# Closing products of the SSD head pairs: issued head by head, or in turn between the two heads

## The chip, the cores and the metric

The kernel runs on one core of one Trainium2 chip. The time is the device time of one execution in microseconds (us). Three runs of the kernel before gave 3219.74, 3220.45 and 3232.57 us, median 3220.45. A further execution was profiled; it took 3218.82 us, of which 3217.0 us lie between its first and its last profiled instruction (the span).

Names used below: PE is the matrix engine (matmuls), PEld its loading of weights, which is recorded apart, DVE the vector engine, ACT the scalar engine, POOL the GpSimd engine, SP the engine that issues most of the transfers.

## The reference, cut to what matters

The program is one inference step of a hybrid decoder layer for 256 prompt tokens and 64 sample tokens (8 sequences of 8), so 320 columns in all, with a model width of 2048, everything in fp32. The layer has a mixer (a state-space scan, SSD, beside a short convolution), attention to 256 memory tokens, and a retrieval of single-neuron experts (PEER). The change lies in the SSD scan. The scan has 32 heads of 64 channels. Within a chunk of 128 tokens each head computes

```
cb     = einsum('bclgn,bcsgn->bgcls', cc, bc)
y_diag = einsum('bgcls,bgrcls,bcsgrp->bclgrp', cb, lmat, xdt)
...
y = (y_diag + y_off)            # y_off: what earlier chunks or the given state add
y = y + d_skip * x
```

`lmat` is a lower triangular matrix of decays for every head. The kernel forms the product of `cb` and `lmat` for a head, 128 source tokens by the target tokens, and multiplies the head's inputs `xdt` (source tokens by 64 channels) with it. That product with `xdt` is what is meant by the closing products of a head.

## The kernel before, in words

**Layout.** Activations lie with channels on the 128 partitions and the 320 token columns along the row. The big projections (`gemm`) split each weight tile into a high and a low part (lines 248 on ACT and 249 on DVE) and multiply three times into one accumulation: lines 367, 368 and 369, each with a 128x128 weight block and 320 moving columns. Weights come by SP's transfers (line 343) into a few rooms, `W`; a room becomes free when line 249 has read it.

**Order of the work.** The order on PE, ACT and DVE is that in which the program is written; there is no scheduler between. A stream (`Stream`) takes the units of the projections one after another; after each unit it advances the side jobs, generators that yield between small pieces of work. The SSD scan (`ssd`, which calls `group(g)` for g = 0 to 3) is such a side job, with 0.7 pieces per unit, while the projections of the mixer run. So each piece of the scan stands on PE between two units of lines 367 to 369, which don't depend on it.

**A group.** A group has 8 heads, taken as 4 pairs (`for j in range(4)`), so there are 16 pairs in all. `XD` holds the heads' inputs with tokens on partitions: `XD[:, 0]` the first 128 prompt tokens, `XD[:, 1]` the next 128, `XD[0:TS, 2]` the 64 sample tokens. `LM` (`lmat`, lines 859 to 862, written on DVE and ACT) holds a head's 128x384 matrix: 128 columns for chunk one onto itself, 128 for chunk one onto chunk two, 128 for chunk two onto itself. `MS` holds the 64x64 matrices of the sample tokens.

**The closing products** of pair j go into one PSUM tile, `py`: the first head into partitions 0 to 63, the second into partitions 64 to 127. Each head has four products: line 906 with 64 rows, 64 weight columns and 64 moving columns (the sample tokens), and lines 907, 908 and 909 with 128 rows, 64 weight columns and 128 moving columns (908 and 909 add up into the same columns). A product of two fp32 operands is recorded as two passes, each with a weight load of its own, so a head has 8 loads and 8 passes, a pair 16. Behind the last product DVE reads `py` once for both heads (line 910).

**A place with the same form of product.** The expert scores of the sample tokens (`scores`, line 1531) multiply 128 rows, 64 weight columns and 128 moving columns too, and there the loop over `r` inside each `j` puts the first product into partitions 0 to 63, the second into 64 to 127, and so on in turn. Both halves get the same operands there:

```
for j, q in enumerate(qs):
    for r in range(2):
        PE.matmul(pt[TS * r:TS * r + TS, j * P:(j + 1) * P], q[:, TP:T], PP["KY"][:, 2 * c + j], start=True, stop=True)
```

Of the kernel before, what the change touches and what calls it, by code (L numbers as in the profile page):

```python
# [19 lines left out]
P = 128  # L20
D = 2048
KC = D // P
TP = 256
TS = 64
T = TP + TS
# [138 lines left out]
def step(ctx, tc, ins, outs, dbg=None, stop=None):  # L164
# [23 lines left out]
    def ps(name="ps"):  # L188
        return psp.tile([P, 512], F32, tag="ps", name=name)

    V, S, G, PE = nc.vector, nc.scalar, nc.gpsimd, nc.tensor
# [47 lines left out]
    def transpose(out, in_):  # L239
        n = in_.shape[0]  # L240
        PE.transpose(out, in_, ident[:n, :n])
# [490 lines left out]
    def ssd():  # L732

        yield from until("decays")
        for g in range(4):
            yield from until("bc", 4 + g)
            yield from wait(2)
            yield from group(g)
# [7 lines left out]
    def group(g):  # L746
# [3 lines left out]
        def bcast(hh):  # L750

            AB = pS.tile([P, 4, T], F32, tag="AB", bufs=1, name="AB")
            h0 = 8 * g + 4 * hh
            nc.gpsimd.dma_start(AB, acs_d[h0:h0 + 4].unsqueeze(0).broadcast_to([P, 4, T]))
            abs_.append(AB)
# [3 lines left out]
        def state_in(j):  # L759
            SB = pS.tile([P, NB, P], F32, tag="SB", bufs=2, name="SB")  # L760
            nc.gpsimd.dma_start(SB, state_ssm[0, :, 8 * g + 2 * j:8 * g + 2 * j + 2].rearrange("b h p n -> (h p) b n"))
            sbs.append(SB)
# [44 lines left out]
        XD = pS.tile([P, 3, 512], F32, tag="XD", bufs=1, name="XD")  # L807
# [37 lines left out]
        def sample_mats(hh):  # L845
            AB, h0 = abs_[hh], 8 * g + 4 * hh
            MS = pS.tile([TS, 4, TS], F32, tag="MS", bufs=2, name="MS")
            V.tensor_tensor(MS, AB[0:TS, :, TP:T], ACN[0:TS, 2, h0:h0 + 4].unsqueeze(2).broadcast_to([TS, 4, TS]),
                            ALU.subtract)
            V.tensor_scalar(MS, MS, 0.0, None, op0=ALU.min)  # L850
            S.activation(MS, MS, AF.Exp)
            V.tensor_tensor(MS, MS, CM[0:TS, 384:448].unsqueeze(1).broadcast_to([TS, 4, TS]), ALU.mult)
            mss.append(MS)

        def lmat(i):

            AB, h, hq = abs_[i // 4], 8 * g + i, i % 4
            LM = pS.tile([P, 384], F32, tag="LM", bufs=3, name="LM")
            V.tensor_scalar(LM[:, 0:TP], AB[:, hq, 0:TP], ACN[:, 0, h:h + 1], 0.0, op0=ALU.subtract, op1=ALU.min)
            V.tensor_scalar(LM[:, TP:384], AB[:, hq, P:TP], ACN[:, 1, h:h + 1], 0.0, op0=ALU.subtract, op1=ALU.min)  # L860
            S.activation(LM, LM, AF.Exp)
            V.tensor_tensor(LM, LM, CM[:, 0:384], ALU.mult)
            lms.append(LM)

        YE = pS.tile([P, 4, TS], F32, tag="YE", bufs=1, name="YE")
        for j in range(4):
            c = 4 * g + j

            SB = sbs[j]
            if j % 2 == 0:  # L870
                sample_mats(j // 2)
            if j == 0:
                bcast(1)
            yield 1
            ST = pS.tile([P, NB, P], F32, tag="ST", bufs=1, name="ST")
            for q in range(2):
                pt = ps("pst")
                for b in range(4):
                    transpose(pt[:, b * P:(b + 1) * P], SB[:, 4 * q + b])
                S.activation(ST[:, 4 * q:4 * q + 4], pt.rearrange("p (b n) -> p b n", n=P), AF.Copy)  # L880
            lmat(2 * j)
            yield 1
            lmat(2 * j + 1)
            yield 1
            YO = ps("YO")
            for b in range(NB):
                PE.matmul(YO[:, LS * b:LS * b + LS], ST[:, b], Cc[:, TP + LS * b:TP + LS * b + LS], start=True, stop=True)
            V.tensor_tensor(YE[:, j], YO[:, 0:TS], EE[:, c], ALU.mult)
            for q in range(2):
                pt = ps("pns")  # L890
                PE.matmul(pt, XQ[:, q, j * P:(j + 1) * P], BD[:, q].rearrange("p b n -> p (b n)"), start=True, stop=True)
                for b in range(4):
                    V.scalar_tensor_tensor(SB[:, 4 * q + b], SB[:, 4 * q + b],
                                           EE[:, c, LS * (4 * q + b) + LS - 1:LS * (4 * q + b) + LS],
                                           pt[:, b * P:(b + 1) * P], ALU.mult, ALU.add)
                yield 1
            nc.gpsimd.dma_start(s_ssm[0, :, 2 * c:2 * c + 2].rearrange("b h p n -> (h p) b n"), SB)
            if j < 2:
                state_in(j + 2)

            py = ps("py")
            for h2 in range(2):
                LM, MS = lms[2 * j + h2], mss[j // 2]
                o = py[64 * h2:64 * h2 + 64]
                d0 = 64 * (2 * j + h2)
                PE.matmul(o[:, TP:T], XD[0:TS, 2, d0:d0 + 64], MS[:, 2 * (j % 2) + h2], start=True, stop=True)
                PE.matmul(o[:, 0:P], XD[:, 0, d0:d0 + 64], LM[:, 0:P], start=True, stop=True)
                PE.matmul(o[:, P:TP], XD[:, 0, d0:d0 + 64], LM[:, P:TP], start=True, stop=False)
                PE.matmul(o[:, P:TP], XD[:, 1, d0:d0 + 64], LM[:, TP:384], start=False, stop=True)
            V.scalar_tensor_tensor(XS[:, c], XS[:, c], DC[:, c:c + 1], py[:, 0:T], ALU.mult, ALU.add)  # L910
            V.tensor_tensor(XS[:, c, TP:T], XS[:, c, TP:T], YE[:, j], ALU.add)
            yield 1
# [1206 lines left out]
```

## Time and profile before

| what | value |
|---|---|
| median of three runs | 3220.45 us (3219.74 to 3232.57) |
| profiled execution, device time | 3218.82 us |
| its span | 3217.0 us |
| PE busy | 3147.9 us, 98% of the span |
| PEld / DVE / ACT / POOL busy | 91% / 73% / 51% / 41% |
| granted PE clock, mean | 0.992 |
| closing products, first to last | 356.3 to 813 us of the span |
| mean transfer rate | 283 GB/s |

How to read it: busy shares are of the whole span. A PE row names the tile sizes as rows*columns of the array (128\*64: 128 rows, 64 columns), then the moving operand. The end of a matmul is modelled, so its recorded length is longer than the time until the next one can start; distances between starts are what a matmul costs in a stream. The time of a stretch on PE is therefore taken here from start to start.

### The profile page before, as it was taken

To read this page: it belongs to the slowest core of one execution; us is meant where nothing else is said; L and a number is where in the kernel's file an instruction comes from. 1 tells how busy PE (TensorE), PEld (TensorE's weight loads), DVE (VectorE), ACT (ScalarE), POOL (GpSimd) and SP (SyncE) were. 2 spreads that over 40 slices of the span, in tenths; PEclk is the share of its full clock that TensorE was granted. 3 is DMA by queue.
4 is the path that set the end of the run, shared out by engine and by line. 5 is a ranking of instruction groups with operands and counts; after the bars stand their busy time and mean duration, and the time that the engine had idled before them with its cause. 6 is when DMAs were issued, how large, how long until landed. Compare 5 with 4: busy or idle time off the path is not lost.

```text
span 3217.0 us, 57525 instructions
## 1 busy us (share of the span) xinstructions
PE 3147.9 (98%) x20589; PEld 2939.2 (91%) x20589; DVE 2339.4 (73%) x4551; ACT 1633.9 (51%) x3219; POOL 1333.5 (41%) x1438
## 2 busy tenths in 40 slices
PE   8999999999999999889999999999999999999997
PEld 7889999999999999769999999999999888888886
DVE  5556866566476557786687899988885788888885
ACT  5545543333454445555445444666665555555554
POOL 0012211111100001231128899988888565556542
PEclk9999999999999999999999999999999999999998
DMA  8668898888999998776676688878998999999995
GB/s 263 208 208 304 276 308 298 297 298 293 315 318 312 309 305 194 212 217 200 182 213 221 228 307 327 309 290 293 329 323 289 322 334 367 327 344 329 334 311 190
DMA packets 475371, 909.29 MB, mean 283 GB/s; under 512 B 40607, under 2 KB 286535, under 8 KB 449572
## 3 DMA queue, kind: packets, MB, share of 16 engines
q1 hardware_dynamic: 352972, 562.95, 52.6%
q0 software_dynamic: 54528, 208.44, 19.0%
q10 hardware_dynamic: 67584, 134.23, 12.4%
q8 instruction: 161, 2.64, 0.3%
q14 instruction: 126, 1.03, 0.1%
HBM read 849.41 MB, written 190.05 MB: 323 GB/s over the span
## 4 chain that ended last, share of the span: by engine, by line
PE 44%; DVE 2%; POOL 1%; issue 1%; DMA 1%; ACT 1%; SPq 0%; DVEq 0%; POOLq 0%; ACTq 0%
PE acc L2021 7%; PE acc L2022 7%; PE acc L2020 7%; PE pu L1867 7%; PE pu L1865 7%; PE pu L1866 7%; PE pgate L1771 2%; POOL L L1849 1%; DVE tt L1837 0%; PE pg L367 0%; PE pg L369 0%; PE pg L368 0%; DVE gu L1729 0%; DMA at<-act_d 0%; ACT junk L2054 0%
## 5 line engine op out<-in xcount | busy, mean ns | idle before, releaser
L249 DVE TENSOR_TENSOR L<-W,H 128x512 fp32r<-128x512 f32 x1320 | 914.8, 717 | 367.9 <-ACT H L248 357.1
L248 ACT ACTIVATE H<-W 128x512 fp32r<-128x512 f32 x1320 | 799.6, 625 | 674.5 <-PE pg L368 230.8
L1849 POOL TENSOR_TENSOR L<-tt,H 128x512 fp32r<-128x512 f32 x509 | 645.9, 1299 | 75.9 <-ACT H L1846 67.1
L367 PE MATMUL pg<-AH,H 128*128 128x320 f32 (+1 forms) x1872 | 587.6, 314 | 0.0
L1865 PE MATMUL pu<-XP,H 128*128 128x256 f32 x2048 | 585.6, 286 | 0.0
L1867 PE MATMUL pu<-XP,L 128*128 128x256 f32 x2048 | 580.6, 283 | 3.7 <-POOL L L1849 3.5
L1866 PE MATMUL pu<-XP,H 128*128 128x256 f32 x2048 | 579.3, 283 | 0.0
L369 PE MATMUL pg<-AH,L 128*128 128x320 f32 (+1 forms) x1872 | 578.7, 309 | 0.0
L368 PE MATMUL pg<-AL,H 128*128 128x320 f32 (+1 forms) x1872 | 578.5, 309 | 0.0
L1837 DVE STREAM_TRANSPOSE tt<-W 128x512 f32<-128x512 f32 x512 | 338.0, 691 | 116.3 <-POOL L L1849 108.9
L2021 PE MATMUL acc<-L,wt 128*128 128x512 f32 x1024 | 398.6, 389 | 0.4 <-DVE L L249 0.4
L2022 PE MATMUL acc<-H,wt 128*128 128x512 f32 x1024 | 398.4, 389 | 0.0
L2020 PE MATMUL acc<-H,wt 128*128 128x512 f32 x1024 | 398.4, 389 | 0.0
L1867 PEld LDWEIGHTS pu<-XP,L 128*128 128x128 f32 x2048 | 392.7, 192 | 5.4 <-POOL L L1849 5.3
L1865 PEld LDWEIGHTS pu<-XP,H 128*128 128x128 f32 x2048 | 393.1, 192 | 0.2 <-ACT xs L1503 0.2
L1866 PEld LDWEIGHTS pu<-XP,H 128*128 128x128 f32 x2048 | 393.1, 192 | 0.0
L1846 ACT ACTIVATE H<-tt 128x512 fp32r<-128x512 f32 x512 | 306.8, 625 | 135.3 <-DVE tt L1837 101.5
L367 PEld LDWEIGHTS pg<-AH,H 128*128 128x128 f32 (+1 forms) x1872 | 350.5, 187 | 4.5 <-issue 2.6
L368 PEld LDWEIGHTS pg<-AL,H 128*128 128x128 f32 (+1 forms) x1872 | 350.6, 187 | 2.3
L369 PEld LDWEIGHTS pg<-AH,L 128*128 128x128 f32 (+1 forms) x1872 | 350.5, 187 | 0.6
L1969 POOL TENSOR_TENSOR at<-at,G 128x108 f32<-128x108 f32 x192 | 151.9, 805 | 259.5 <-DMA at<-act_d 195.1
L2021 PEld LDWEIGHTS acc<-L,wt 128*128 128x128 f32 x1024 | 192.2, 188 | 41.0 <-DVE L L249 1.2
(489 smaller groups left out, 5330.1 us busy)
## 6 DMA issues: line engine op xcount, KB each, us to landing
u_d<-in_peer_u_dram ACTq DMA_DIRECT2D x128, 1024.0 KB, 7.8
W<-u_d SPq DMA_DIRECT2D x128, 1024.0 KB, 6.1
W<-in_peer_v_dram SPq DMA_DIRECT2D x256, 512.0 KB, 6.3
W<-in_w_in_dram SPq DMA_DIRECT2D x176, 512.0 KB, 6.8
W<-in_w_out_dram SPq DMA_DIRECT2D x64, 512.0 KB, 7.2
W<-in_w_mem_k_dram SPq DMA_DIRECT2D x32, 512.0 KB, 7.0
W<-in_w_mem_v_dram SPq DMA_DIRECT2D x32, 512.0 KB, 4.6
W<-in_w_mem_q_dram SPq DMA_DIRECT2D x32, 512.0 KB, 7.1
```

The costliest lines, as they stand in the source:

```text
L248: S.activation(h, src, AF.Copy)
L249: V.tensor_tensor(l, src, h.bitcast(F32), ALU.subtract)
L367: PE.matmul(out, hv[:, j, c0:c1], ah[:, k, 0:n], start=st, stop=False)
L368: PE.matmul(out, hv[:, j, c0:c1], al[:, k, 0:n], start=False, stop=False)
L369: PE.matmul(out, lv[:, j, c0:c1], ah[:, k, 0:n], start=False, stop=sp)
L1849: G.tensor_tensor(l, src, h.bitcast(F32), ALU.subtract)
L1865: PE.matmul(pu[:, 0:TP], hv[:, j], PP["xp"][:, 0, k], start=k == 0, stop=False)
L1866: PE.matmul(pu[:, 0:TP], hv[:, j], PP["xp"][:, 1, k], start=False, stop=False)
L1867: PE.matmul(pu[:, 0:TP], lv[:, j], PP["xp"][:, 0, k], start=False, stop=k == KC - 1)
L2020: PE.matmul(out, th, h, start=i == 0, stop=False)
L2021: PE.matmul(out, th, l, start=False, stop=False)
L2022: PE.matmul(out, tl, h, start=False, stop=i == P - 1)
```

## The change

The four products of each head are first written into a list, the 64-row product last. Then the two lists are walked side by side: one product of the first head, the same one of the second, and so on. Operands, outputs and start and stop marks are the same as before.

```diff
             py = ps("py")
+            parts = []
             for h2 in range(2):
                 LM, MS = lms[2 * j + h2], mss[j // 2]
                 o = py[64 * h2:64 * h2 + 64]
-                d0 = 64 * (2 * j + h2)
-                PE.matmul(o[:, TP:T], XD[0:TS, 2, d0:d0 + 64], MS[:, 2 * (j % 2) + h2], start=True, stop=True)
-                PE.matmul(o[:, 0:P], XD[:, 0, d0:d0 + 64], LM[:, 0:P], start=True, stop=True)
-                PE.matmul(o[:, P:TP], XD[:, 0, d0:d0 + 64], LM[:, P:TP], start=True, stop=False)
-                PE.matmul(o[:, P:TP], XD[:, 1, d0:d0 + 64], LM[:, TP:384], start=False, stop=True)
+                x = XD[:, :, 64 * (2 * j + h2):64 * (2 * j + h2) + 64]
+                parts.append(((o[:, 0:P], x[:, 0], LM[:, 0:P], True, True),
+                              (o[:, P:TP], x[:, 0], LM[:, P:TP], True, False),
+                              (o[:, P:TP], x[:, 1], LM[:, TP:384], False, True),
+                              (o[:, TP:T], x[0:TS, 2], MS[:, 2 * (j % 2) + h2], True, True)))
+            for pair in zip(*parts):
+                for o, w, m, first, last in pair:
+                    PE.matmul(o, w, m, start=first, stop=last)
             V.scalar_tensor_tensor(XS[:, c], XS[:, c], DC[:, c:c + 1], py[:, 0:T], ALU.mult, ALU.add)
             V.tensor_tensor(XS[:, c, TP:T], XS[:, c, TP:T], YE[:, j], ALU.add)
```

On PE, at the first of the 16 pairs, between two units of a projection, the order with its waits was this (`py` is the tile of the closing products, `XD` holds the weights, `MS` and `LM` are moving; a name such as DVE_49 is the counter of an engine that is waited for):

```order
L369 MATMUL pg_3699<-AH,L 128x320
L906 MATMUL py<-MS,XD 64x64 [waits PE_49]
L907 MATMUL py<-LM,XD 64x128
L908 MATMUL py<-LM,XD 64x128
L909 MATMUL py<-LM,XD 64x128
L906 MATMUL py<-MS,XD 64x64
L907 MATMUL py<-LM,XD 64x128 [waits DVE_49]
L908 MATMUL py<-LM,XD 64x128
L909 MATMUL py<-LM,XD 64x128
L367 MATMUL pg_3698<-AH,H 128x320 [waits Activation_49]
```

At the same place of the changed kernel it is this:

```order
L369 MATMUL pg_3699<-AH,L 128x320
L913 MATMUL py<-LM,XD 64x128 [waits PE_49]
L913 MATMUL py<-LM,XD 64x128 [waits DVE_49]
L913 MATMUL py<-LM,XD 64x128 x4
L913 MATMUL py<-MS,XD 64x64 x2
L367 MATMUL pg_3698<-AH,H 128x320 [waits Activation_49]
```

All eight products stand at the same line now, the six with 128 rows ahead of the two with 64, and the wait for DVE (for the second head's `LM`) stands at the second product instead of the sixth. Nothing else moved on PE, and the order on DVE, ACT, POOL and SP is the same row by row.

## The prediction, made before the changed kernel ran

> **What bounds the kernel now.** I read the page first, for the share of each engine.
>
> ```profile
> span 3217.0 us, 57525 instructions
> ...
> PE 3147.9 (98%) x20589; PEld 2939.2 (91%) x20589; DVE 2339.4 (73%) x4551; ACT 1633.9 (51%) x3219; POOL 1333.5 (41%) x1438
> ```
>
> PE is busy for 98% of the span. That alone doesn't say that PE sets the time where the change lies, so next come the groups that touch the tile `py`, for where and how often, and the busy time by windows around it (PE, PEld, DVE, ACT, POOL, then granted PE clock, DMA share, GB/s).
>
> ```profile
> L906 PEld LDWEIGHTS py<-MS,XD x64: 129/132/133, 356.3 to 812.0; 64*64 64x64 f32 x64
> ...
> L909 PE MATMUL py<-LM,XD x64: 272/273/273, 357.0 to 812.8; 128*64 128x128 f32 x64
> L910 DVE SCALAR_TENSOR_TENSOR XS<-XS,DC,py x16: 541/547/548, 362.1 to 813.1; 128x320 f32<-128x320 f32 x16
> ...
>   PE py L909: 26.6, 11
> ```
>
> ```profile
> 350.00:815.00 465.00, 464.97 (x3277) 451.09 (x3277) 296.54 (x672) 190.48 (x358) 75.48 (x165) 1.00 0.89 298
> 815.00:1250.00 435.00, 431.34 (x2958) 428.46 (x2958) 261.30 (x465) 212.46 (x390) 24.92 (x42) 1.00 0.94 304
> ```
>
> There are 16 pairs (one read by line 910 for each), all between 356 and 813 us. In the 465 us around them PE is busy for 464.97, at full granted clock. The list of waits for that stretch has no row for PE; these are ACT's and SP's longest:
>
> ```profile
> ACT H L248 <- PE pg L368: 118.0, 76, 3.4
> ```
>
> ```profile
> SPq L343 <- DVE L L249: 408.9, 101, 11.1
> SPq L343 <- DVE MS L848: 6.8, 3, 3.2
> SPq L343 <- DMA W<-in_w_in_dram: 4.3, 2, 2.5
> ```
>
> ACT waits 118 us for PE to release a split tile, and SP waits 408.9 us for room for the next weights, only 4.3 us for a transfer. Everything that feeds PE is ahead of it. So here a microsecond taken from PE is a microsecond taken from the path.
>
> **What a pair costs now.** The timeline of PE at the first pair, and two rows of the last:
>
> ```profile
> 355.90 0.31 PE L368 MATMUL pg<-AL,H 128*128 128x320 f32 x1
> 356.05 0.31 PE L369 MATMUL pg<-AH,L 128*128 128x320 f32 x1
> 356.29 0.33 PE L906 MATMUL py<-MS,XD 64*64 64x64 f32 x2
> 356.55 0.43 PE L907 MATMUL py<-LM,XD 128*64 128x128 f32 x2
> 356.81 0.38 PE L908 MATMUL py<-LM,XD 128*64 128x128 f32 x2
> 357.03 0.38 PE L909 MATMUL py<-LM,XD 128*64 128x128 f32 x2
> 357.35 0.33 PE L906 MATMUL py<-MS,XD 64*64 64x64 f32 x2
> ...
> 358.09 0.38 PE L909 MATMUL py<-LM,XD 128*64 128x128 f32 x2
> 358.40 0.41 PE L367 MATMUL pg<-AH,H 128*128 128x320 f32 x1
> 358.65 0.31 PE L368 MATMUL pg<-AL,H 128*128 128x320 f32 x1
> ```
>
> ```profile
> 810.84 0.33 PE L906 MATMUL py<-MS,XD 64*64 64x64 f32 x2
> ...
> 812.95 0.41 PE L367 MATMUL pg<-AH,H 128*128 128x320 f32 x1
> ```
>
> From the first closing product to the next projection the first pair takes 358.40 - 356.29 = 2.11 us, the last one 812.95 - 810.84 = 2.11 as well. 16 x 2.11 = 33.8 us is all that the change can touch. Three prices are in these rows. Line 908 to line 909 is 0.22 us for two passes, so **one pass in a stream is 0.11 us**. The other two need the weight loads:
>
> ```profile
> 356.71 0.25 PEld L908 LDWEIGHTS py<-LM,XD 128*64 128x64 f32 x2
> ...
> 357.34 0.19 PEld L906 LDWEIGHTS py<-MS,XD 64*64 64x64 f32 x2 [0.17 <-issue]
> 357.60 0.19 PEld L907 LDWEIGHTS py<-LM,XD 128*64 128x64 f32 x2
> ...
> 358.40 0.19 PEld L367 LDWEIGHTS pg<-AH,H 128*128 128x128 f32 x1 [0.17 <-issue]
> ```
>
> Two loads of line 906 take 0.19 us and one takes 0.13, so **loads follow each other by 0.06**. Inside one form a load is hidden: line 908's starts at 356.71, while line 907's passes run. Where the form changes (64\*64, 128\*64, 128\*128) it isn't: the last passes of line 909 begin at 357.03 and are through after two times 0.11, at 357.25, yet the next load starts at 357.34, 0.09 later, and its pass has to wait for it. **A change of form costs 0.09 + 0.06 = 0.15 us.** The 128-row part of a head is thus 357.34 - 356.55 = 0.79 us (0.06 + 6 x 0.11 + 0.09, rounded), the 64-row part 356.55 - 356.29 = 0.26.
>
> **The change, part by part.** *64 rows last.* A pair goes through five changes of form now (in, 64 to 128, back to 64, 128 again, out), and through three afterwards. Two fewer, in 16 pairs: 2 x 0.15 x 16 = 4.8 us. The way in (0.24 from line 369 at 356.05) and out (0.25 to the next start) has a change from and to 128\*128 as before, and stays.
>
> *In turn between the halves.* The closing products show no two neighbours in different halves without a change of form between them. Line 1531 does, in the same form: eight passes of 128\*64 by 128 columns, halves in turn.
>
> ```profile
> 1632.26 0.30 PE L369 MATMUL pg<-BH,L 128*128 128x320 f32 x1
> 1632.49 0.42 PEld L1531 LDWEIGHTS pscs<-KY,q 128*64 128x64 f32 x8 [0.19 <-issue]
> 1632.49 0.66 PE L1531 MATMUL pscs<-KY,q 128*64 128x128 f32 x8
> 1633.08 0.19 PEld L367 LDWEIGHTS pg<-BH,H 128*128 128x128 f32 x1 [0.17 <-issue]
> ```
>
> ```profile
> 1587.97 0.66 PE L1531 MATMUL pscs<-KY,q 128*64 128x128 f32 x8
> 1588.56 0.41 PE L367 MATMUL pg<-BH,H 128*128 128x320 f32 x1
> ```
>
> From its start to the next form: 1633.08 - 1632.49 = 0.59 us, at the other place 0.59 too. One half after another, eight passes would take 0.79 + 2 x 0.11 = 1.01. In place of that stand four slots: 0.06 + 4 x 0.11 + 0.09 = 0.59. So two passes share each slot, loads included.
>
> Bounds for the pair. *Nothing shared:* 12 passes with 128 rows take 0.79 + 6 x 0.11 = 1.45, the 64-row part gets two more passes of half the columns, 0.26 + 2 x 0.055 = 0.37; together 1.82, saving 0.29 (4.6 us over 16 pairs). *All shared:* six slots, 0.59 + 2 x 0.11 = 0.81, and a 64-row part of 0.27 (0.01 for the second half's later start, an estimate); together 1.08, saving 1.03. *A loss:* each of the six changes of half that happen within a form costs as much as a change of form, 6 x 0.15 - 0.29 = 0.61 us more (9.8 over 16). I take all shared, since line 1531 has the same form, loads and passes: **16 x 1.03 = 16.5 us.**
>
> What line 1531 doesn't show is halves with different operands: there both read the same `q` and `KY`, here each head has its own. The projections suggest that the reading allows it: they stream 320 columns from start to start in 0.15 us (355.90 to 356.05), 2.1 columns a ns, and two passes of 128 columns in a 0.11 slot need 2.3. The Trainium skill, page "TensorEngine Tiling (Array Packing)", section "Key Properties", says that different tiles of the array can load weights and multiply at the same time and that changing the tiling mode, not the tile, drains the array; by it the sum stays at 16.5 us. No run here yet shows it for different operands.
>
> *Waits.* The wait for the second head's `LM` moves up to the second product, about 1.3 us earlier. The latest piece of `LM` ahead of the first pair:
>
> ```profile
> 352.69 0.56 DVE L862 TENSOR_TENSOR LM<-LM,CM 128x384 f32<-128x384 f32 x1 [0.59 <-ACT LM L861]
> ```
>
> It is done at 353.25, 3.0 us before the first product, so the wait finds it there. Line 910 on DVE, which waited 26.6 us in 11 cases for the last product, gets `py` earlier; DVE is off the path.
>
> *Does the gain last?* The stretch would have 465 - 16.5 = 448.5 us for the same transfers, a DMA share of 0.89 x 465 / 448.5 = 0.92; behind it 0.94 is carried at nearly full PE. DVE would be at 296.54 / 448.5 = 66%. What follows starts earlier, in the same order. I count the gain in full: 3218.82 - 16.5 = 3202.3 for a profiled execution. The median lay 1.63 above that execution, so **3204.0 us** as a median.
>
> **The rivals.**
> *A. The halves share only when they read the same.* Then only the changes of form go: 3220.45 - 4.6 = 3215.9. For it: line 1531's operands are the same. Against it: its loads and passes are recorded one by one for both halves, and the reading rate above. 10%.
> *B. Loads are no longer hidden* once both halves run: each of six slots grows by a load of 0.06, 16 x 0.36 = 5.8 us of the gain are lost, 3220.45 - 10.7 = 3209.8. Line 1531 speaks against it, with eight loads within four slots of 0.11. 5%. The Trainium skill has such a rule, page "TensorE: Matmul & The Clock Gate", section "The mechanism" of its part 3: a load overlaps a running matmul only if their row groups differ, and both halves use all rows. The trace doesn't agree: line 908's load runs under line 907's passes in the very same half.
> *C. The weights become the bound.* If the transfers can't go above a share of 0.90 here, the stretch needs 0.89 x 465 / 0.90 = 460 us, and only 5 us are gained: 3215.4. Against it: SP's 4.3 us of waiting for transfers, and 0.94 in the stretch behind. 6%.
> *D. Slower.* A change of half drains the array like a change of form; with the loss above, 3220.45 + 9.8 = 3230.2. It decides from 0.29 / 6 = 0.05 us for one change of half. Against it are line 1531's 0.59 us, which hold three such changes from product to product. 4%.
>
> **How the numbers follow.** All shared has 75%, and its own range is 3201 to 3208: two of the three runs lie 0.7 us apart and the third 12 above, so a median of three can be off by a few us, and a little may be lost later. A measurement here can tell about 0.5%, which is 16.1 us. The forecast of 16.5 is 0.51% and lies on that line, so its 75% are split nearly in half, 39% beyond it and 36% within. A, B and C lie within, and so does D at its price of 0.3%; only a dearer D would be beyond it, 2%. That makes 39% faster, 59% the same, 2% slower. For 8 in 10 the range takes in the likeliest case with some scatter below, and B, C and A above: 3199 to 3217; D is left out.
>
> **What would show it.** Right: from the first row of line 913 to the next row of line 367 some 1.08 us instead of 2.11 in each of the 16 places; the starts of the two heads' passes a hundredth of a us apart; PE still without a wait between 350 and 800 us; the mixer's last closing product 16 us earlier. 1.82 us would show A, about 1.44 B, 2.7 D; waits of PE for `H` or `L`, with ACT waiting for `W`, would show C. The forecast is wrong if the pair stays above 1.5 us, or if the pair shrinks and the end doesn't follow.

## The result and the profile after

The changed kernel takes 3208.92 us (median of 9 runs, 3202.56 to 3216.41), the kernel before 3223.89 (median of 9, 3219.74 to 3232.57). The ratio is 0.995, with a 95% interval from 0.9936 to 0.9965: faster by 15.0 us, 0.5%. The ratio and its interval are worked out from the single runs and are not exactly the quotient of the two medians. The profiled execution of the changed kernel took 3211.91 us, with a span of 3210.1. The time of an execution tends to go with its mean granted PE clock: of the nine of the changed kernel the two at 0.992 average 3202.7 us, the two at 0.989 average 3213.6; the profiled one had 0.989, that of the kernel before 0.992.

The timeline of PE at the first and at the last pair of the changed kernel:

```profile
356.39 0.31 PE L369 MATMUL pg<-AH,L 128*128 128x320 f32 x1
356.63 0.88 PE L913 MATMUL py<-LM,XD 128*64 128x128 f32 x12
357.44 0.33 PE L913 MATMUL py<-MS,XD 64*64 64x64 f32 x4
357.70 0.41 PE L367 MATMUL pg<-AH,H 128*128 128x320 f32 x1
357.95 0.31 PE L368 MATMUL pg<-AL,H 128*128 128x320 f32 x1
...
795.49 0.88 PE L913 MATMUL py<-LM,XD 128*64 128x128 f32 x12
796.29 0.33 PE L913 MATMUL py<-MS,XD 64*64 64x64 f32 x4
796.55 0.41 PE L367 MATMUL pg<-AH,H 128*128 128x320 f32 x1
```

The first pair takes 357.70 - 356.63 = 1.07 us in place of 2.11: 0.81 for the twelve passes with 128 rows, 0.26 for the four with 64. The way in (0.24) and out (0.25) is as before. The last pair takes 1.06, and starts 810.84 - 795.49 = 15.35 us earlier; the first one started 0.34 later, so the 15 pairs between them have saved 15.7, or 1.05 each. The stretch around them by windows, its waits of ACT and of SP, and the wait on the tile `py`:

```profile
350.00:815.00 465.00, 464.97 (x3394) 454.67 (x3394) 306.09 (x690) 196.91 (x369) 76.43 (x171) 1.00 0.91 307
```

```profile
ACT H L248 <- PE pg L368: 106.1, 74, 3.2
...
ACT H L248 <- DMA W<-in_w_in_dram: 12.1, 7, 3.2
```

```profile
SPq L343 <- DVE L L249: 403.2, 106, 11.1
SPq L343 <- DMA W<-in_w_in_dram: 7.8, 5, 3.3
```

```profile
  PE py L913: 15.2, 11
```

PE is still busy throughout, at full granted clock; the share of the transfers rose from 0.89 to 0.91. ACT waits 12.1 us for transfers (2.2 before, from 350 to 820 us) and SP 7.8 (4.3 before), but ACT still waits 106 us for PE, and PE has no wait in this stretch. DVE waits 15.2 us for `py` in place of 26.6.

The gain of 15.35 us at the last pair became only 3217.0 - 3210.1 = 6.9 us at the end of this profiled execution. The first attention product of the sample tokens (line 1317 before, 1321 after) shows how much of it was lost on the way there:

```profile
L1317 PE MATMUL pss<-KH,qm x128: 274/278/474, 1218.3 to 1424.3; 128*64 128x256 f32 x128
```

```profile
L1321 PE MATMUL pss<-KH,qm x128: 274/279/476, 1208.1 to 1415.8; 128*64 128x256 f32 x128
```

It starts 10.2 us earlier, so 5 us were lost before it; the other 3.3 went behind it, and where is not shown. In between PE has gaps, by its timeline, and ACT's waits from 1120 to 1200 us point to the cause of most of them:

```profile
1155.26 0.41 PE L367 MATMUL pg<-AH,H 128*128 128x320 f32 x1 [1.19 <-ACT H L248]
...
1170.50 0.42 PE L367 MATMUL pg<-AH,H 128*128 128x320 f32 x1 [0.46 <-ACT H L248]
```

```profile
ACT H L248 <- DMA W<-in_w_out_dram: 22.1, 3, 9.3
```

A tile of output weights came up to 9.3 us late, and PE ran dry some 360 us behind the last pair. Whether the change brings that about or chance is asked of the first experiment.

### The profile page after: what moved, and what is told of

It reads as the page before. It is cut to its first block, busy times and chain, and to the rows that moved or that the text cites. A ratio compares the mean times of both kernels' runs of the same rounds, so it can differ in the third digit from the quotient of the medians.

```text
span 3210.1 us, 57528 instructions
## 1 busy us (share of the span) xinstructions
PE 3138.9 (98%) x20589; PEld 2930.0 (91%) x20589; DVE 2336.8 (73%) x4551; ACT 1631.5 (51%) x3219; POOL 1343.9 (42%) x1438
## 3 DMA queue, kind: packets, MB, share of 16 engines
q8 instruction: 161, 2.64, 0.3%
## 4 chain that ended last, share of the span: by engine, by line
PE 43%; DVE 2%; POOL 2%; issue 1%; DMA 1%; ACT 1%; DVEq 0%; POOLq 0%; SPq 0%; ACTq 0%
PE acc L2025 7%; PE acc L2026 7%; PE acc L2024 7%; PE pu L1871 6%; PE pu L1869 6%; PE pu L1870 6%; PE pgate L1775 2%; POOL L L1853 1%; DVE tt L1841 0%; PE pg L367 0%; PE pg L369 0%; PE pg L368 0%; DMA act_d<-at 0%; DVE gu L1733 0%; DVE L L249 0%
## 5 line engine op out<-in xcount | busy, mean ns | idle before, releaser
L1973 POOL TENSOR_TENSOR at<-at,G 128x108 f32<-128x108 f32 x192 | 165.3, 874 | 256.9 <-DMA at<-act_d 214.6
```

## Experiments

Each run is timed against runs of the kernel before on the same chip. Pairs are measured in the trace from the first closing product to the next projection; within a kernel the 16 pairs agree to 0.01 us.

### The changed kernel again

Nothing is edited.

> The changed kernel once more, nothing edited. Theory (the gain on PE reaches the end, and the 6 us that the first profiled execution lost between 1155 and 1190 us were a weight transfer that happened to land late): every pair 1.07 us from its first closing product to the next projection, the last pair about 15 us earlier than before; a loss of that size at the same place need not come back, and the median is 15 to 17 us under before. Rival (the shorter mixer makes the last weights of the output projection late each time): PE waits some 5 us at the same place again, and the median is about 9 us under before.

3205.94 us (median of 7) against 3225.45 (of 15), ratio 0.9951 (0.9934 to 0.9968). The last pair and the first attention product of this run:

```profile
794.95 0.88 PE L913 MATMUL py<-LM,XD 128*64 128x128 f32 x12
795.76 0.33 PE L913 MATMUL py<-MS,XD 64*64 64x64 f32 x4
796.02 0.41 PE L367 MATMUL pg<-AH,H 128*128 128x320 f32 x1
```

```profile
L1321 PE MATMUL pss<-KH,qm x128: 274/279/473, 1199.9 to 1405.4; 128*64 128x256 f32 x128
```

```profile
ACT H L248 <- DMA W<-in_w_out_dram: 7.2, 3, 4.2
```

The pair is the same. The late weights are not there (7.2 us of waiting for them, 10.6 in the kernel before from 1120 to 1200 us), the attention starts 18.4 us earlier than before, and the span is 3198.8, 18.2 shorter. The runs below with another order of the closing products bear it out: in none of their profiles does PE wait at line 367 between 820 and 1320 us, and ACT's longest wait for these weights is 5.6 us. So the loss in the first profiled execution needn't come with the change. Executions of one kernel spread over 9 to 22 us where there are seven or more (3200.62 to 3219.95 here, 3217.06 to 3234.82 before), and the two profiled ones of the changed kernel are 11.3 us apart; the medians show gains of 15.0 and 19.5 us.

### All closing products twice

```diff
-            for h2 in range(2):
+            for h2 in (0, 1, 0, 1):
```

in the kernel before.

> The kernel before with all closing products of a pair issued twice, the second time with the same result: 2.11 us more on PE in each of 16 places, 33.7 us in all, and nothing else. Theory (in this stretch each microsecond on PE is one of the whole time): 33.7 us slower than before, ratio 1.0105, and PE still without waits there. Rival (part of PE's time there is cover for transfers and would be waited for anyway): clearly less than 30 us slower.

3259.58 us (median of 4), 34.1 more than before, ratio 1.011 (1.0091 to 1.0129); from 350 to 850 us PE is busy for 499.98 of 500. The first pair of this run starts and ends here:

```profile
355.54 0.33 PE L906 MATMUL py<-MS,XD 64*64 64x64 f32 x2
...
359.45 0.38 PE L909 MATMUL py<-LM,XD 128*64 128x128 f32 x2
359.76 0.41 PE L367 MATMUL pg<-AH,H 128*128 128x320 f32 x1
```

4.22 us in place of 2.11. 33.7 us added on PE are 34.1 at the end (29 to 42 by the interval): in this stretch a microsecond on PE is one of the whole, as near as the runs can tell.

### The heads one after another, 64 rows last

```diff
-            for pair in zip(*parts):
-                for o, w, m, first, last in pair:
-                    PE.matmul(o, w, m, start=first, stop=last)
+            for o, w, m, first, last in parts[0][:3] + parts[1][:3] + (parts[0][3], parts[1][3]):
+                PE.matmul(o, w, m, start=first, stop=last)
```

in the changed kernel; `parts[0]` are the first head's products, `parts[1]` the second's.

> One part of the change alone: the 64-row products last, so three changes of form in a pair in place of five, but all three 128-row products of the first head ahead of those of the second. Theory (products start in the order of issue, and two run at once only where neighbours write different halves): only the last product of the first head and the first of the second run together; 0.06 + 5 products x 0.22 + 0.09 = 1.25 us for the 128-row part and 0.26 for the 64-row part, 1.51 a pair, saving 0.60, 9.6 us in all. Rival 1 (PE looks ahead and finds the other half's products by itself; what stood in the way before was the change of form between the heads): 1.07 a pair, 16.6 us in all, as with the whole change. Rival 2 (no overlap without strict turns, only the two changes of form saved): 1.72 to 1.82 a pair, 5 to 6 us in all.

3213.98 us (median of 9) against 3225.45, ratio 0.9963 (0.9949 to 0.9977). A pair:

```profile
354.78 1.14 PE L912 MATMUL py<-LM,XD 128*64 128x128 f32 x12
355.85 0.33 PE L912 MATMUL py<-MS,XD 64*64 64x64 f32 x4
356.11 0.42 PE L367 MATMUL pg<-AH,H 128*128 128x320 f32 x1
```

1.34 us by unrounded times, which no theory had: 2.108 - 1.336 = 0.77 saved, 12.4 us over the 16 pairs, three quarters of the whole change without any turn between neighbours. One head alone takes 0.79 for its 128-row part, both take 355.85 - 354.78 = 1.07, so the second head began 0.28 us after the first (its first pass starts 0.275 us after in the trace). That is when the first head's first product is through (0.06 + 2 x 0.11), with two more of its products still ahead of the second head in the order. From this came a new theory: each half holds one product at work and one waiting, and the issue stops only at a third for the same half.

### Two and two

```diff
+            for o, w, m, first, last in parts[0][:2] + parts[1][:2] + parts[0][2:3] + parts[1][2:] + parts[0][3:]:
```

> Two 128-row products of the first head, two of the second, then one and one, then the 64-row ones. Theory, formed after the run with the heads one after another (there the second head began 0.27 us after the first, just when the first head's first product was through): each half holds one product at work and one waiting, and the issue stops only at a third. Then two and two is no worse than strict turns, 1.07 us a pair, the second head 0.01 behind the first. Rival (the 0.27 was the time to issue two further products at 0.13 each): the second head begins 0.13 later, about 1.20 a pair.

```profile
357.82 0.88 PE L912 MATMUL py<-LM,XD 128*64 128x128 f32 x12
358.63 0.33 PE L912 MATMUL py<-MS,XD 64*64 64x64 f32 x4
358.89 0.41 PE L367 MATMUL pg<-AH,H 128*128 128x320 f32 x1
```

1.07 us a pair, as with strict turns; 0.81 for the 128-row part leaves the second head 0.01 to 0.02 behind the first (0.013 in the trace). (One run, 3209.87 us, against 3221.4.)

### Six and six

```diff
+            for o, w, m, first, last in 2 * parts[0][:3] + 2 * parts[1][:3] + (parts[0][3], parts[1][3]):
```

> The three 128-row products of the first head twice over, then those of the second twice over (with the same result), then the 64-row ones: a longer run in one half. Theory (one at work and one waiting in each half): the second head begins when the fourth product of the first is through, 0.06 + 4 x 0.22 = 0.93 us after it, and a pair takes 0.93 + 0.06 + 6 x 0.22 + 0.09 + 0.26 = 2.65 us. Rival 1 (0.13 us to issue each product): it begins 5 x 0.13 = 0.67 after, 2.39 a pair. Rival 2 (a long look ahead): 0.27 after or less, 2.0 a pair or less.

```profile
359.00 2.45 PE L912 MATMUL py<-LM,XD 128*64 128x128 f32 x24
361.38 0.33 PE L912 MATMUL py<-MS,XD 64*64 64x64 f32 x4
361.64 0.41 PE L367 MATMUL pg<-AH,H 128*128 128x320 f32 x1
```

2.64 us a pair (2.646 by unrounded times) where one at work and one waiting gives 2.65, and the rivals 2.39 and 2.0. In the trace the second head's first pass starts 0.930 us after the first head's; the theory had 0.93. (One run, 3232.15 us against 3221.4: 16 x 0.54 = 8.6 us were added on PE.)

The runs in blocks of three, two and six would also fit one limit of three products for both halves together. The changed kernel's own trace speaks against that: the second head's second product begins to load its weights 0.17 us after the pair's first pass, while the first head's first product, through at 0.27, is still at work and its second has begun to load, so four products are in hand, two in each half. Whether the limit counts products or passes, of which each product here has two, is not told apart.

### The 64-row products between the heads

```diff
+            for o, w, m, first, last in parts[0] + parts[1][3:] + parts[1][:3]:
```

> The three 128-row products of the first head, then the two 64-row products, then the three of the second head. Theory (products of two halves run at once only without a change of form between them): no 128-row pass of the two heads shares a slot; 0.79 + 0.26 + 0.79 = 1.84 us a pair, 0.27 less than before the change. Rival (PE looks past the change of form): about 1.34, as where the heads' 128-row products stood next to each other.

```profile
358.79 0.87 PE L912 MATMUL py<-LM,XD 128*64 128x128 f32 x6
359.59 0.33 PE L912 MATMUL py<-MS,XD 64*64 64x64 f32 x4
359.85 0.87 PE L912 MATMUL py<-LM,XD 128*64 128x128 f32 x6
360.65 0.42 PE L367 MATMUL pg<-AH,H 128*128 128x320 f32 x1
```

0.80, 0.26 and 0.80, together 1.86: no 128-row passes of the two heads share a slot, while the two 64-row products, neighbours in two halves, do. (One run, 3216.8 us against 3221.4; 4.0 us less on PE.) With the run of the heads one after another (1.34, 128-row products next to each other) this shows what held the heads apart before the change: the second head's 64-row product between them. In these runs a change of form is a wall that the look ahead doesn't pass.

### 64 rows first

```diff
-            for pair in zip(*parts):
+            for pair in sorted(zip(*parts), key=lambda p: p[0][1].shape[0]):
```

> The halves in turn as in the change, but the two 64-row products first, as before the change. Theory (where the 64-row products stand doesn't matter, since a pair has three changes of form either way): 1.07 us a pair, 16.6 us less in all, the same time as the changed kernel. Rival (a way from 64*64 straight to the projections' 128*128 is cheaper or dearer than from 128*64): a pair differs by up to 0.1 us, 1.6 us in all.

3210.2 us (median of 6) against 3225.45, ratio 0.9956 (0.9942 to 0.997).

```profile
358.15 0.33 PE L913 MATMUL py<-MS,XD 64*64 64x64 f32 x4
358.41 0.88 PE L913 MATMUL py<-LM,XD 128*64 128x128 f32 x12
359.21 0.41 PE L367 MATMUL pg<-AH,H 128*128 128x320 f32 x1
```

1.07 us by unrounded times, as in the changed kernel: that the 64-row kind comes last is worth nothing; that both of them stand together is.

### One form for all: zero rows

```diff
         XE = pS.tile([P, 2, 512], F32, tag="XE", bufs=1, name="XE")
+        G.memset(XD[TS:P, 2], 0.0)
...
-            MS = pS.tile([TS, 4, TS], F32, tag="MS", bufs=2, name="MS")
+            full = pS.tile([P, 4, TS], F32, tag="MS", bufs=2, name="MS")
+            G.memset(full[TS:P], 0.0)
+            MS = full[0:TS]
...
-            mss.append(MS)
+            mss.append(full)
...
-                              (o[:, TP:T], x[0:TS, 2], MS[:, 2 * (j % 2) + h2], True, True)))
+                              (o[:, TP:T], x[:, 2], MS[:, 2 * (j % 2) + h2], True, True)))
```

> The changed kernel with the 64-row products made 128 rows deep: the upper 64 rows of their weights and of MS are set to zero by POOL (4 and 8 small fills in all), which adds exact zeros. So a pair has two changes of form in place of three. Theory (a change of form costs 0.15 us, a slot of a 64-column pass 0.055): 1.07 - 0.26 + 2 x 0.055 = 0.92 us a pair, 2.4 us less in all than the changed kernel; the time itself can't show so little. Rival (the fills come late, and PE or DVE wait for POOL): the pairs shrink, but PE waits appear ahead of them and the last pair comes no earlier than in the changed kernel.

3201.95 us (median of 6) against 3221.4 (of 11), ratio 0.9929 (0.9909 to 0.9948): the lowest median of all, though its interval overlaps that of the changed kernel.

```profile
357.49 0.88 PE L916 MATMUL py<-LM,XD 128*64 128x128 f32 x12
358.20 0.28 PE L916 MATMUL py<-MS,XD 128*64 128x64 f32 x4
358.41 0.42 PE L367 MATMUL pg<-AH,H 128*128 128x320 f32 x1
...
794.14 0.88 PE L916 MATMUL py<-LM,XD 128*64 128x128 f32 x12
```

0.92 us a pair as forecast; from the first pair to the last it is 436.65 us, against 438.86 in the changed kernel, 2.2 less over 15 pairs, and PE has no wait between them. So 16 x 0.148 = 2.4 us less than in the changed kernel are shown on PE. Against the kernel before it is 16 x 1.188 = 19.0 us on PE, and the medians differ by 19.4; the time alone can't tell this kernel from the changed one. DVE has no wait for POOL in the stretch, so the fills don't come late.

## Why the prediction was right, and where not

**What bounds the kernel** held: PE has no wait in the stretch, and 33.7 us added there came out as 34.1.

**The price of a pair** held to a hundredth: 0.81 + 0.26 = 1.07, forecast 1.08. (The working writes 0.79 for one head's 128-row part and adds it up from 0.06 + 6 x 0.11 + 0.09, which is 0.81; by unrounded times it is 0.80.) Line 1531, from another place of the same trace, gave it. The 0.01 for the second half's later start was put in without a row behind it; the trace has 0.007. The one gap of line 1531, that both halves read the same operands there, turned out not to matter: with different operands two passes share a slot too. That settles rival A. The Trainium skill, page "TensorEngine Tiling (Array Packing)", section "Key Properties", says that different tiles of the array can load weights and multiply in parallel; the trace agrees. Rival B, loads that are no longer hidden, fell too: twelve loads go into a 128-row part of 0.81 us, which is six slots of 0.11 and the 0.15 around them. The rule of the Trainium skill, page "TensorE: Matmul & The Clock Gate", section "The mechanism", that a load overlaps a running matmul only where the row groups differ, does not hold here.

**Waits and transfers** held: the wait for the second head's `LM` costs nothing, and from 350 to 798.5 us, the stretch that the forecast meant, the transfers' share was 0.92, as forecast, without PE waiting, so rival C fell. Rival D fell with the price of a pair.

**The time.** 3204.0 was forecast, 3208.92 came. Most of the difference is the starting point: the median of three runs was 3220.45, that of nine is 3223.89, 3.4 higher, and the profiled execution of before lay lower still. The gain was put at 16.5 us; the medians of the two measurements give 15.0 and 19.5, and the intervals of their ratios run from 11 to 21 us and from 10 to 21. On PE the 16 pairs took 16 x 1.041 = 16.7 us less.

**What was mis-sized is the share of the two parts.** The text gave 64 rows last 4.8 us, for two saved changes of form, and the rest of the 16.5 to the turns. The heads one after another, with the same changes of form, save 12.4; the turns add the other 4.3. The price of a change of form wasn't wrong: with zero rows, one fewer saves 0.148 us a pair, where 0.15 was forecast. What the working left out is that the two changes of form also kept the heads apart: once none stands between them, PE overlaps them by itself, except for the first head's lead. The sum of 16.5 didn't depend on the split, so it came out right all the same.

**The gain afterwards.** That it lasts to the end was right for the medians. The first profiled execution kept 6.9 of its 15.35 us: 5 were lost ahead of the attention, most of them where weights came late far behind the change, and 3.3 after it. Why the weights were late in that execution is open.

## What to carry to other kernels

Where a product uses only half of the array's columns, look for a neighbour for the other half; strict turns aren't needed as long as no more than two products in a row go into one half. Keep products of another form out of such a run, or bring them to the same form with zero rows: here the product in between cost more by keeping the halves apart than by its own change of form. And before the two profiled executions are compared, compare the stretch that was changed: single executions scatter by as much as such a change is worth.

## What was not expected of the hardware

PE starts products out of the order in which they are issued, but only a little: in runs of three products for each half the second half began 0.28 us after the first, in runs of six 0.93, in runs of two 0.01. That fits one product at work and one waiting in each half of the columns. A product of another form in between ends it: 0.80 and 0.80 one after the other, with the 64-row part of 0.26 between them.
